# FFN inner units in three parts, and one pool of 4 KB buffers for weights and activations

## The chip, the cores and the metric

The kernel runs on one core of a Trainium2 chip. The metric is the device time of one execution in microseconds (us); of the kernel before there are three timed runs and one profiled execution. The engines are PE (TensorE: matrix products), PEld (its weight loads, which overlap PE), DVE (VectorE), ACT (ScalarE), POOL (GpSimd) and SP (SyncE, which here issues the DMAs).

## What is computed

A trunk of two layers over 256 latent tokens (stream L) and 256 context tokens (stream C) of 1024 features. Each layer is a feed forward, a token mixer (retention in layer 0, 2-D neighbourhood attention in layer 1) and a second feed forward:

```python
def ada_in(h, g, m, j):
    xn = rms_norm(h, g)
    return xn * (1.0 + m[:, j, 1][:, None]) + m[:, j, 0][:, None]

def gated_residual(h, m, j, y, w):
    return h + w * m[:, j, 2][:, None] * y

def swiglu(x, w_in, w_out):                 # w_in 1024 x 5632, w_out 2816 x 1024
    a, b = jnp.split(x @ w_in, 2, axis=-1)
    return (jax.nn.silu(a) * b) @ w_out

for i in range(2):
    h = gated_residual(h, ml, 0, swiglu(ada_in(h, norm_g[i, 0], ml, 0), ffn_w_in[i, 0], ffn_w_out[i, 0]), 0.5)
    ...
    h = gated_residual(h, ml, 1, yl, 1.0)   # yl: the mixer
    ...
    h = gated_residual(h, ml, 2, swiglu(ada_in(h, norm_g[i, 2], ml, 2), ffn_w_in[i, 1], ffn_w_out[i, 1]), 0.5)
return rms_norm(h, final_norm_g)
```

The context stream hc goes through the same steps with its own modulation (`mc`) and the same weights, up to the keys and values of layer 1's mixer. The output is the latent stream.

## The kernel before

**Stages.** `trunk()` lays the work out in one order, by hand: start-up (0 to 57 us of the profiled execution), FFN0 (57 to 412), retention (412 to 800), FFN1 (800 to 1192), FFN2 (1192 to 1555), neighbourhood mixer (1555 to 1750), FFN3 on the latent stream alone (1750 to 1945), final norm. All activations are kept transposed, features on the partitions, so that a product has 512 columns for both streams or 256 for one.

**Products.** Each matrix product is made as three: a weight and an activation are each split into a high part (a cast to fp32r, on ACT) and a low part (the rest, a subtraction on DVE), and PE adds up high·high, high·low and low·high (`acc3`, `acc3_part`, `mm`, which is the line L259 of the profile). L151 is the helper through which every instruction of DVE, ACT and POOL goes.

**Weights.** `plan` lists the weight tiles in the order of their use. `load()` issues a tile's DMA into a `raw` buffer, `prep()` queues the split into `whi` (ACT) and `wlo` (DVE) in two halves, `weight()` takes a tile, `retire()` gives its buffers back, and `pump()` starts what the free buffers allow. `wpool` has 2 `raw`, 3 `whi` and 3 `wlo` buffers of 8 KB per partition; activations live in 24 `slots` of 4 KB (160 KB in all).

**A feed forward** (`ffn`) goes over the 2816 inner units as 22 chunks of 128 in two parts of `HALF` = 11. In a part, 11 `win` tiles are multiplied (48 products each: `a` and `b` halves of the chunk, 8 k-blocks, 3 terms), each followed by silu, product and split (`gated_part`), and then 8 `wout` tiles, one for each output block n of 128 features, with 11 x 3 products each. `finish` adds an output block to h (`residual`: a DVE operation `h<-one,gate,h` for each stream); in the last part it is followed by the square of the new h (ACT) for the next norm.

**The hand-over.** In the last part of FFN0, FFN1 and FFN2 the blocks n = 6 and 7 are multiplied for one stream at a time, with 256 columns: L6, L7, C6, C7. When L7 is done, `chain` brings the L stream to the next stage: h, its square, the sum of the squares over the features (a product with a matrix of ones, 128x2, "rows product"), eight small DVE operations for the reciprocal root (`few`), two diagonal matrices (DVE), a product that spreads them over the partitions (128x128, "diagonal product"), and for each k-block of 128 features a scaled h on DVE (`t<-h,scl,one`), its high part on ACT and its low part on DVE (`slot<-t,modT,slot`). Meanwhile PE multiplies C6 and C7. Then the same follows for C, while PE multiplies the next stage's first products with L.

**Order.** Steps off the path are put in queues (`later`, `soon`, `due`), from which `advance()`, called after each product, takes what is due by a planner's clock `now`. The modulation of all layers (`bg`: `acc<-mraw,sT,acc` on DVE) runs in the background, one step for each `BG_EVERY` = 2.2 us.

Of the kernel before, what the change touches and what calls it, by code (L numbers as in the profile page):

```python
# [9 lines left out]
F32 = mybir.dt.float32  # L10
F32R = mybir.dt.float32r
# [13 lines left out]
HALF = NHC // 2  # L25
# [4 lines left out]
H_RET = 4  # L30
BIG = 1e30

# [39 lines left out]
def trunk(ctx, tc, a):  # L72
# [4 lines left out]
    slots = ctx.enter_context(tc.tile_pool(name="slots", bufs=24))  # L77
# [111 lines left out]

    plan = []  # L190

    def plan_all():
        for f in range(2):
            for hf in range(2):
                plan.extend(a["win"][f, hf * HALF + t] for t in range(HALF))
                plan.extend(a["wout"][f, hf, n] for n in range(KC))
            if f == 0:
                for hd in range(H_RET):
                    plan.extend([a["rq"][hd], a["rk"][hd], a["rv"][hd, 0], a["rv"][hd, 1]])
                    if hd:  # L200
                        plan.extend([a["ro"][hd - 1, 0], a["ro"][hd - 1, 1]])
                    plan.extend([a["rg"][hd, 0], a["rg"][hd, 1]])
                plan.extend([a["ro"][H_RET - 1, 0], a["ro"][H_RET - 1, 1]])
        for f in range(2, 4):
            for hf in range(2):
                plan.extend(a["win"][f, hf * HALF + t] for t in range(HALF))
                plan.extend(a["wout"][f, hf, n] for n in range(KC))
            if f == 2:
                for g in range(4):
                    plan.extend([a["nq"][g], a["nk"][g], a["nv"][g]])  # L210
                plan.extend(a["no"][n] for n in range(4))

    plan_all()
    RAWS, SPLITS = 2, 3
    raws, split_tiles = [], []
    state = {"loaded": 0, "freed": 0, "split": 0, "retired": 0, "bg_at": 0.0, "hold": True, "sums": True, "inside": True, "lag": (0.0, 0.0), "tight": False}
# [11 lines left out]
    def advance():  # L228
# [4 lines left out]
        while soon and not state["tight"] and soon[0][0] <= now["pe"] and ready_at(soon[0][5]) <= now["pe"] + 0.3 and free("dve", 0.5):  # L233
            soon.pop(0)[2]()
# [34 lines left out]
    def load():  # L269
        src = plan[state["loaded"]]  # L270
# [1301 lines left out]
```

## Time and profile before

| | us |
|---|---|
| timed runs, median of 3 (lowest to highest) | 1951.85 (1951.35 to 1952.06) |
| profiled execution, its own time | 1952.25 |
| its span | 1950.2 |
| PE busy | 1924.2 |
| DVE busy | 1352.0 |
| ACT busy | 687.9 |

The profiled execution is 0.40 us above the median, and 2.05 us of its time lie around the span. PE's busy time counts matmuls whose ends overlap the next one's start; starts of successive products tell the cadence better than the lengths.

### The profile page before, as it was taken

What the parts mean: (1) busy time and instruction counts of PE and PEld (TensorE: products, weight loads), DVE (VectorE), ACT (ScalarE), POOL (GpSimd) and SP (SyncE); (2) the same over time, 40 slices, a digit from 0 to 9 for tenths busy, and PEclk for the clock granted to TensorE, in tenths of its full rate; (3) what the DMA queues carried; (4) which work ended last, traced back from release to release, by engine and by line L of the source; (5) the groups of instructions that cost most, each with busy time, mean ns of one, the idle gap of its engine ahead of it and who ended that gap; (6) DMA issues with size and microseconds to landing.
All of it is one profiled execution on the core that took longest, in us unless ns stands there. A gap on an engine that the chain in (4) does not pass through costs nothing.

```text
span 1950.2 us, 26148 instructions
## 1 busy us (share of the span) xinstructions
PE 1924.2 (99%) x10458; PEld 1661.8 (85%) x10458; DVE 1352.0 (69%) x2402; ACT 687.9 (35%) x1035; POOL 73.0 (4%) x108
## 2 busy tenths in 40 slices
PE   7999999999999999999999999999999999999998
PEld 4888888898888888888888889888888899989998
DVE  5576666678788888876666676767632588887665
ACT  5422232333323232342222223322222366665443
POOL 1000000010000000100000000000000101100000
PEclk8999999999999999999999999999999999999999
DMA  7334534434434434234353343555433345544553
GB/s 287 141 137 129 187 130 136 156 119 151 142 133 141 147 130 142 86 130 149 125 179 132 140 139 98 194 189 200 162 101 82 110 119 113 98 115 167 194 176 114
DMA packets 70090, 278.85 MB, mean 143 GB/s; under 512 B 23632, under 2 KB 23888, under 8 KB 52304
## 3 DMA queue, kind: packets, MB, share of 16 engines
q1 hardware_dynamic: 69968, 277.18, 43.5%
q8 instruction: 82, 1.34, 0.3%
q14 instruction: 40, 0.33, 0.0%
HBM read 276.11 MB, written 1.05 MB: 142 GB/s over the span
## 4 chain that ended last, share of the span: by engine, by line
PE 94%; DVE 3%; ACT 2%; DMA 1%; issue 0%; SPq 0%; DVEq 0%; ACTq 0%
PE pair L259 61%; PE one L259 32%; DVE slot L151 1%; PE one L265 1%; DMA slot<-in_wmod 1%; DVE t L151 1%; ACT slot L151 1%; DVE wlo L151 1%; ACT whi L151 1%; DVE few L151 0%; DMA raw<-in_nv 0%; ACT t L151 0%; DVE h L151 0%; PE pair L265 0%; SPq L166 0%
## 5 line engine op out<-in xcount | busy, mean ns | idle before, releaser
L259 PE MATMUL pair<-slot,whi 128*128 128x512 f32 (+2 forms) x4000 | 1039.1, 351 | 6.8 <-ACT slot L151 4.7
L259 PEld LDWEIGHTS pair<-slot,whi 128*128 128x128 f32 x4000 | 696.4, 190 | 104.3 <-ACT slot L151 5.4
L259 PE MATMUL pair<-slot,wlo 128*128 128x512 f32 (+2 forms) x2000 | 682.5, 350 | 0.1
L259 PE MATMUL one<-slot,whi 128*128 128x512 f32 (+1 forms) x1860 | 481.4, 347 | 0.0
L151 DVE TENSOR_TENSOR wlo<-raw,whi 128x1024 fp32r<-128x1024 f32 (+1 forms) x400 | 436.4, 1122 | 38.5 <-ACT whi L151 37.7
L151 ACT CAST whi<-raw 128x1024 fp32r<-128x1024 f32 (+1 forms) x400 | 365.0, 959 | 225.3 <-PE one L259 138.6
L259 PEld LDWEIGHTS pair<-slot,wlo 128*128 128x128 f32 x2000 | 372.9, 190 | 48.8 <-DVE wlo L151 0.4
L259 PEld LDWEIGHTS one<-slot,whi 128*128 128x128 f32 x1860 | 325.9, 189 | 43.4
L259 PE MATMUL one<-slot,wlo 128*128 128x512 f32 (+1 forms) x930 | 323.1, 347 | 0.0
L151 DVE SCALAR_TENSOR_TENSOR acc<-mraw,sT,acc 128x512 f32<-128x512 f32 x392 | 279.2, 750 | 17.1 <-DMA mraw<-in_wmod 15.9
L151 ACT ACTIVATE t<-pair 128x512 f32<-128x512 f32 x66 | 39.4, 597 | 442.9 <-PE pair L259 442.9
L259 PEld LDWEIGHTS one<-slot,wlo 128*128 128x128 f32 x930 | 176.1, 189 | 21.8
L151 DVE TENSOR_TENSOR t<-pair,t 128x512 f32<-128x512 f32 x66 | 45.6, 692 | 204.2 <-ACT t L151 204.2
L151 DVE TENSOR_TENSOR slot<-t,slot 128x512 fp32r<-128x512 f32 (+2 forms) x144 | 88.1, 612 | 64.8 <-ACT slot L151 63.4
L151 ACT CAST slot<-t 128x512 fp32r<-128x512 f32 (+2 forms) x144 | 79.4, 552 | 122.1 <-DVE t L151 121.7
L151 DVE SCALAR_TENSOR_TENSOR h<-one,gate,h 128x256 f32<-128x256 f32 x112 | 49.6, 479 | 103.6 <-PE one L259 103.4
L151 POOL TENSOR_TENSOR t<-t,t 128x256 f32<-128x256 f32 x47 | 39.4, 850 | 1708.4 <-ACT t L151 1286.9
L259 PE MATMUL pair<-whi,slot 128*128 128x512 f32 (+1 forms) x384 | 98.5, 339 | 0.0
L259 PE MATMUL one<-slot,slot 128*128 128x512 f32 (+1 forms) x432 | 89.8, 348 | 1.3 <-DVE slot L151 1.0
L151 ACT ACTIVATE t<-h 128x256 f32<-128x256 f32 (+1 forms) x88 | 36.9, 434 | 142.8 <-DVE h L151 129.3
L259 PEld LDWEIGHTS one<-slot,slot 128*128 128x128 f32 x432 | 69.9, 189 | 10.8 <-DVE slot L151 1.4
L259 PEld LDWEIGHTS pair<-whi,slot 128*128 128x128 f32 x384 | 67.2, 189 | 7.5
(100 smaller groups left out, 1077.8 us busy)
## 6 DMA issues: line engine op xcount, KB each, us to landing
raw<-in_win SPq DMA_DIRECT2D x88, 1024.0 KB, 4.9
mraw<-in_wmod SPq DMA_DIRECT2D x128, 512.0 KB, 4.7
raw<-in_wout SPq DMA_DIRECT2D x64, 704.0 KB, 4.2
slot<-in_wmod SPq DMA_DIRECT2D x16, 512.0 KB, 10.3
raw<-in_rv SPq DMA_DIRECT2D x8, 1024.0 KB, 4.8
raw<-in_rg SPq DMA_DIRECT2D x8, 1024.0 KB, 4.9
raw<-in_ro SPq DMA_DIRECT2D x8, 1024.0 KB, 4.9
slot<-in_ex SPq DMA_DIRECT2D x8, 512.0 KB, 6.0
```

Source lines behind the costliest of these rows:

```text
L151: getattr(self.real, op)(*args, **kw)
L259: nc.tensor.matmul(out, lhsT=lhsT, rhs=rhs, start=start, stop=stop)
L265: nc.tensor.transpose(out=out, in_=in_, identity=ident)
```

## The change

The inner units of each feed forward go in three parts of 8, 7 and 7 chunks (`PARTS`) in place of two of 11. A part has again 8 output blocks, so each FFN adds to h three times, and the blocks of the last part have 7 x 3 products in place of 11 x 3. `wpool`'s weight buffers are gone: `slots` has 40 buffers of 4 KB (again 160 KB), shared by raw tiles (`RAWS` = 4 units at a time), split weights (`SPLITS` = 12) and activations. A `win` tile is loaded as two DMAs of 512 KB, a `wout` tile as one of 512 or 448 KB (the host lays `wout` out by chunk); SP issues 599 DMAs in place of 431.

The change brings a second way to multiply a tile (`Seven`, `product`, `seven`, `low_by_dma`), taken where `in_seven` is true. With `STANDARD` = (22, 22, 22) it is true for no tile. `operands(xt)`, which prepares the sums of activations that `seven` would read, is called in the last part of FFN0, FFN1 and FFN2 (`t1 == standard`), and nothing reads what it makes: in each FFN 8 additions of 512 columns, 3 combinations and 4 low parts of 1024 columns on DVE, and 4 casts of 1024 columns on ACT.

Two smaller edits: the background modulation takes one step for each 1.2 us until the block (0, C, 5) is made, and 2.2 us after that; `mcol` makes a missing modulation block on demand.

```diff
-HALF = NHC // 2
+PARTS = ((0, 8), (8, 15), (15, 22))
...
+SLOTS, RAWS, SPLITS = 40, 4, 12
...
+STANDARD, AMONG = (22, 22, 22), (2, 3, 3)
...
-    slots = ctx.enter_context(tc.tile_pool(name="slots", bufs=24))
+    slots = ctx.enter_context(tc.tile_pool(name="slots", bufs=SLOTS))
...
+    def in_seven(f, t):
+        return f < 3 and t >= STANDARD[f] and (t - STANDARD[f]) % AMONG[f] < AMONG[f] - 1
...
+    def plan_ffn(f):
+        for p, (t0, t1) in enumerate(PARTS):
+            for t in range(t0, t1):
+                if in_seven(f, t):
+                    plan.append(("seven", [a["wrow"][f, t, r] for r in range(2)]))
+                else:
+                    plan.append(("plain", halves(a["win"][f, t])))
+            plan.extend(("plain", [a["wout"][f, n][:, t0:t1, :]]) for n in range(KC))
...
         if not state["hold"] and now["pe"] >= state["bg_at"] and free("dve", 0.2):
-            state["bg_at"] = max(state["bg_at"], now["pe"] - 4 * BG_EVERY) + BG_EVERY
+
+            every = BG_EVERY if (0, C, 5) in made else 1.2
+            state["bg_at"] = max(state["bg_at"], now["pe"] - 4 * every) + every
             next(bg, None)
...
+        units = []
+        for src in srcs:
+            n = src.shape[1] * src.shape[2]
+            t = slots.tile([P, 1024], F32, tag="slot", name=nm("raw"))
+            dma(out=t[:, :n].rearrange("p (k c) -> p k c", k=src.shape[1]), in_=src)
+            units.append(t)
...
+    def part_tile():
+        return slots.tile([P, 1024], F32R, tag="slot", name=nm("wp"))
...
+    def operands(xt):
...
+        whole(0, L)
+        whole(0, C)
+        whole(1, C)
+        combine(1, (0, L), "minus", (0, L), (0, C))
+        two(1)
+        combine(3, (0, C), "minus", (1, C), (0, C))
+        combine(2, (1, C), "opposite", 1, (1, C))
+        two(2)
+        whole(1, L)
+        two(3)
+        combine(4, (1, L), "opposite", 2, (1, L))
+        two(4)
...
-        for hf in range(2):
+        for hf, (t0, t1) in enumerate(PARTS):
             gts = []
+            size, final = t1 - t0, hf == len(PARTS) - 1
...
+            if not raw and t1 == standard:
+                made_operands = operands(xt)
...
-            last = KC - 2 if hf == 1 and len(streams) == 2 else KC
+            last = KC - 2 if final and len(streams) == 2 else KC
...
                     for n, w in zip((KC - 2, KC - 1), ws):
                         ps = one()
-                        acc3(ps[:, xc], terms(w, xc, range(HALF)))
+                        acc3(ps[:, xc], terms(w, xc, range(size)))
```

By the instruction order, PE has 10278 matmuls in place of 10350: in each of FFN0, FFN1 and FFN2 48 products of 256 columns have become 24 of 512, since fewer of them are made for one stream alone. The columns multiplied are the same in all.

PE, where FFN0 hands over to retention. Before, `one_3095` is C7 (block 7 of stream C), and the diagonal product `one_3108` is put behind the first 4 of its 33 products:

```order
L259 MATMUL one_3095<-slot_1838,whi_2893 128x256 x2
L259 MATMUL one_3095<-slot_1838,wlo_2894 128x256
L259 MATMUL one_3095<-slot_1910,whi_2893 128x256
L259 MATMUL one_3108<-t_428_3071,con 128x128 x2
L259 MATMUL one_3095<-slot_1910,whi_2893 128x256
L259 MATMUL one_3095<-slot_1910,wlo_2894 128x256
L259 MATMUL one_3095<-slot_1991,whi_2893 128x256 x2
L259 MATMUL one_3095<-slot_1991,wlo_2894 128x256
```

After, `one_3243` is C7; its last products, the diagonal product `one_3303`, and then retention's first product `pair_3293`:

```order
L283 MATMUL one_3243<-slot_2812,wp_2970 128x256 x2
L283 MATMUL one_3243<-slot_2812,wp_2971 128x256
L283 MATMUL one_3243<-slot_2890,wp_2970 128x256 x2
L283 MATMUL one_3243<-slot_2890,wp_2971 128x256
L283 MATMUL one_3303<-t_551_3262,con 128x128 x2
L283 MATMUL pair_3293<-slot_3295,wp_3052 128x256
L283 MATMUL pair_3293<-slot_3296,wp_3052 128x256
L283 MATMUL pair_3293<-slot_3295,wp_3053 128x256
```

Before, 29 products of C7 stood behind the diagonal product; now none does, and 16 stand between the rows product and the diagonal product.

DVE, the same place. Before: from block 5 (`one_2901`) over L6 (`one_2956`) and L7 (`one_2998`) to the reciprocal root (`few`):

```order
L151 SCALAR_TENSOR_TENSOR h_84<-one_2901,gate_1441,h_84 128x256
L151 SCALAR_TENSOR_TENSOR h_85<-one_2901,gate_1443,h_85 128x256
L151 TENSOR_TENSOR wlo_2949<-raw_2878,whi_2948 128x1024
L151 SCALAR_TENSOR_TENSOR h_84<-one_2956,gate_1441,h_84 128x256
L151 TENSOR_TENSOR wlo_2949<-raw_2878,whi_2948 128x1024
L151 SCALAR_TENSOR_TENSOR h_84<-one_2998,gate_1441,h_84 128x256
L151 TENSOR_TENSOR t_372_2682<-t_423_3037,t_372_2682 128x256
L151 TENSOR_SCALAR few_3061<-one_3058 128x2
```

After: the same stretch, from block 5 (`one_3098`) over L6 (`one_3151`), L7 (`one_3181`) and C6 (`one_3212`); `slot_3118` and `slot_3130` belong to `operands`, `wp_3142` and `wp_3144` are low parts of weights:

```order
L161 SCALAR_TENSOR_TENSOR h_84<-one_3098,gate_1256,h_84 128x256
L161 SCALAR_TENSOR_TENSOR h_85<-one_3098,gate_1268,h_85 128x256
L161 TENSOR_TENSOR slot_3130<-slot_2937,slot_3129 128x1024
L161 SCALAR_TENSOR_TENSOR h_84<-one_3151,gate_1256,h_84 128x256
L161 SCALAR_TENSOR_TENSOR slot_3118<-slot_2946,slot_3118 128x1024
L161 TENSOR_TENSOR wp_3142<-raw_3107,wp_3141 128x1024
L161 SCALAR_TENSOR_TENSOR h_84<-one_3181,gate_1256,h_84 128x256
L161 TENSOR_TENSOR t_495_2962<-t_542_3210,t_495_2962 128x256
L161 TENSOR_TENSOR wp_3144<-raw_3109,wp_3143 128x1024
L161 SCALAR_TENSOR_TENSOR h_85<-one_3212,gate_1268,h_85 128x256
L161 TENSOR_SCALAR few_3252<-one_3249 128x2
```

An operation of `operands` and the low part of a weight now stand ahead of L7's `h_84`, and a weight's low part and C6's `h_85` ahead of `few`.

PE, where FFN1 hands over to FFN2. Before, `one_9315` is C7 and `one_9328` the diagonal product:

```order
L259 MATMUL one_9315<-slot_8069,whi_9113 128x256 x2
L259 MATMUL one_9315<-slot_8069,wlo_9114 128x256
L259 MATMUL one_9315<-slot_8147,whi_9113 128x256
L259 MATMUL one_9328<-t_1291_9291,con 128x128 x2
L259 MATMUL one_9315<-slot_8147,whi_9113 128x256
L259 MATMUL one_9315<-slot_8147,wlo_9114 128x256
L259 MATMUL one_9315<-slot_8227,whi_9113 128x256 x2
```

After, `one_9716` is C7, `one_9745` the diagonal product and `pair_9766` FFN2's first product:

```order
L283 MATMUL one_9716<-slot_9282,wp_9442 128x256 x2
L283 MATMUL one_9716<-slot_9282,wp_9443 128x256
L283 MATMUL one_9716<-slot_9362,wp_9442 128x256
L283 MATMUL one_9745<-t_1612_9709,con 128x128 x2
L283 MATMUL one_9716<-slot_9362,wp_9442 128x256
L283 MATMUL one_9716<-slot_9362,wp_9443 128x256
L283 MATMUL pair_9766<-slot_9737,wp_9518 128x256
L283 MATMUL pair_9766<-slot_9738,wp_9518 128x256
```

Before, 29 products of C7 stood behind the diagonal product; now 2 do. FFN2 into the neighbourhood mixer has the same form.

## Rows read from the trace of the kernel before

**Rows 1.** The page: span, engines and the granted clock in 40 slices.

```profile
span 1950.2 us, 26148 instructions
...
PE 1924.2 (99%) x10458; PEld 1661.8 (85%) x10458; DVE 1352.0 (69%) x2402; ACT 687.9 (35%) x1035; POOL 73.0 (4%) x108
...
PEclk8999999999999999999999999999999999999999
```

**Rows 2.** Windows: from:to, length, busy time (instructions) by engine, granted clock, DMA share, GB/s.

```profile
0.00:57.00 57.00, 45.82 (x197) 25.72 (x198) 31.50 (x66) 28.32 (x41) 8.61 (x29) 0.88 0.68 259
...
243.00:352.00 109.00, 109.00 (x485) 90.27 (x484) 70.68 (x116) 29.67 (x40) 0.00 (x0) 1.00 0.39 134
1555.00:1755.00 200.00, 194.93 (x1425) 182.45 (x1424) 167.90 (x342) 127.07 (x236) 26.70 (x35) 1.00 0.49 109
...
1847.00:1907.00 60.00, 60.00 (x499) 60.00 (x498) 40.10 (x62) 28.01 (x42) 0.00 (x0) 1.00 0.54 178
```

**Rows 3.** Timeline of PE, FFN0 into retention: start, length, instruction and count.

```profile
404.70 0.40 PE L259 MATMUL one<-slot,whi 128*128 128x256 f32 x2
...
406.74 0.51 PE L259 MATMUL one<-con,t 128*128 128x2 f32 x4
...
409.58 0.60 PE L259 MATMUL one<-t,con 128*128 128x128 f32 x4
...
413.49 0.40 PE L259 MATMUL pair<-slot,whi 128*128 128x256 f32 x2
```

**Rows 4.** Timeline of DVE, the same stretch, with idle time before and releaser.

```profile
404.90 0.48 DVE L151 SCALAR_TENSOR_TENSOR h<-one,gate,h 128x256 f32<-128x256 f32 x1 [2.34 <-PE one L259]
406.00 0.43 DVE L151 TENSOR_TENSOR t<-t,t 128x256 f32<-128x256 f32 x1 [0.61 <-ACT t L151]
407.28 0.16 DVE L151 TENSOR_SCALAR few<-one 128x2 int32<-128x2 int32 x1 [0.86 <-PE one L259]
...
410.22 0.87 DVE L151 SCALAR_TENSOR_TENSOR t<-h,scl,one 128x256 f32<-128x256 f32 x2 [0.36 <-PE one L259]
...
413.70 0.49 DVE L151 SCALAR_TENSOR_TENSOR h<-one,gate,h 128x256 f32<-128x256 f32 x1 [0.35 <-PE one L259]
...
417.85 0.48 DVE L151 SCALAR_TENSOR_TENSOR slot<-t,modT,slot 128x256 fp32r<-128x256 f32 x1 [0.18 <-ACT slot L151]
```

**Rows 5.** Timeline of ACT, the same stretch: the square of h.

```profile
405.48 0.42 ACT L151 ACTIVATE t<-h 128x256 f32<-128x256 f32 x1 [3.54 <-DVE h L151]
```

**Rows 6.** Timeline of DVE, FFN1 into FFN2.

```profile
1183.30 0.49 DVE L151 SCALAR_TENSOR_TENSOR h<-one,gate,h 128x256 f32<-128x256 f32 x1 [2.34 <-PE one L259]
...
1196.23 0.48 DVE L151 SCALAR_TENSOR_TENSOR slot<-t,modT,slot 128x256 fp32r<-128x256 f32 x1 [0.18 <-ACT slot L151]
```

**Rows 7.** Groups by line and shape: count, busy us, mean ns, idle before, releasers.

```profile
L151 DVE TENSOR_TENSOR wlo<-raw,whi 128x1024 fp32r<-128x1024 f32 x272 | 324.3, 1222 | 21.5 <-ACT whi L151 21.0
L151 DVE SCALAR_TENSOR_TENSOR acc<-mraw,sT,acc 128x512 f32<-128x512 f32 x392 | 279.2, 750 | 17.1 <-DMA mraw<-in_wmod 15.9
...
L151 DVE TENSOR_TENSOR slot<-t,slot 128x512 fp32r<-128x512 f32 x98 | 67.8, 692 | 56.8 <-ACT slot L151 56.3
...
L151 DVE SCALAR_TENSOR_TENSOR h<-one,gate,h 128x256 f32<-128x256 f32 x112 | 49.6, 479 | 103.6 <-PE one L259 103.4
...
L151 DVE TENSOR_TENSOR slot<-slot,slot 128x1024 fp32r<-128x1024 f32 x10 | 11.8, 1219 | 1.5 <-ACT slot L151 1.4
```

**Rows 8.** The page: the DMA issue of win, and weight loads of PE on low parts.

```profile
L259 PEld LDWEIGHTS pair<-slot,wlo 128*128 128x128 f32 x2000 | 372.9, 190 | 48.8 <-DVE wlo L151 0.4
...
raw<-in_win SPq DMA_DIRECT2D x88, 1024.0 KB, 4.9
```

**Rows 9.** Windows, columns as in rows 2: start of the kernel, neighbourhood into FFN3.

```profile
40.00:50.00 10.00, 9.06 (x36) 5.76 (x35) 10.00 (x11) 6.28 (x8) 0.00 (x0) 0.61 0.00 0
...
1733.00:1755.00 22.00, 18.02 (x136) 16.44 (x135) 19.66 (x52) 12.88 (x32) 1.62 (x2) 1.00 0.28 96
```

**Rows 10.** Timeline of DVE near the end of the neighbourhood mixer.

```profile
1738.52 2.34 DVE L151 TENSOR_TENSOR wlo<-raw,whi 128x1024 fp32r<-128x1024 f32 x2
```

More of the change, by code (lines that the diff above doesn't have):

```diff
@@ new lines, in plan_all @@
+    def plan_all():
+        two = lambda *srcs: plan.extend((MIXED and "mixed" or "plain", halves(x)) for x in srcs)
+        plan_ffn(0)
+        for hd in range(H_RET):
+            two(a["rq"][hd], a["rk"][hd], a["rv"][hd, 0], a["rv"][hd, 1])
+            if hd:
+                two(a["ro"][hd - 1, 0], a["ro"][hd - 1, 1])
+            two(a["rg"][hd, 0], a["rg"][hd, 1])
+        two(a["ro"][H_RET - 1, 0], a["ro"][H_RET - 1, 1])
+        plan_ffn(1)
+        plan_ffn(2)
+        for g in range(4):
+            two(a["nq"][g], a["nk"][g], a["nv"][g])
+        two(*(a["no"][n] for n in range(4)))
+        plan_ffn(3)
@@ L232, in advance @@
         go(later[L])
-        while soon and not state["tight"] and soon[0][0] <= now["pe"] and ready_at(soon[0][5]) <= now["pe"] + 0.3 and free("dve", 0.5):
+        while soon and not state["tight"] and soon[0][0] <= now["pe"] and ready_at(soon[0][5]) <= now["pe"] + 0.3 and free("dve", 0.5) and state["parts"] + soon[0][6] <= SPLITS:
             soon.pop(0)[2]()
@@ L277, in prep, with landed @@
+    def landed(n):
+        state["raw"] -= n
+        pump()
     def prep():
[L278 removed]
+        kind, units, srcs = raws.pop(0)
         tile_no = state["split"]
         state["split"] += 1
[L281 to L296 removed]
@@ L300, in pump, with released @@
+    def released(n):
+        state["parts"] -= n
+        pump()
     def pump():
         while True:
-            if raws and state["split"] - state["retired"] < SPLITS:
+            if raws and (not split_tiles if raws[0][0] == "seven" else
+                         state["parts"] + 2 * len(raws[0][1]) <= state["limit"] and not any(x[6] for x in soon)):
                 prep()
-            elif state["loaded"] < len(plan) and state["loaded"] - state["freed"] < RAWS:
+            elif state["loaded"] < len(plan) and state["raw"] + len(plan[state["loaded"]][1]) <= RAWS:
@@ L446, in mcol @@
         c0 = (j * 3 + w) * KC
-        assert all((l, v, (c0 + k) // 4) in made for k in range(kk.start, kk.stop))
+        while not all((l, v, (c0 + k) // 4) in made for k in range(kk.start, kk.stop)):
+            if due:
+                mod_sum(*due.pop(0)[1])
+            else:
+                next(bg, None)
         return modT[:, l, v, c0 + kk.start:c0 + kk.stop]
@@ L782, in ffn @@
                 state["hold"] = False
-            for t in range(len(gts), HALF):
+            for t in range(len(gts), size):
+                if t0 + t == standard:
+                    x7 = made_operands()
+                    state["limit"] = SPLITS
+                if in_seven(2 * l + which, t0 + t):
+                    gts.append(slot([P, 2, 512], F32R))
+                    seven(t, gts[t], x7)
+                    continue
+                if not raw and t0 + t == standard - 3 and standard < PARTS[0][1]:
+                    made_operands = operands(xt)
+                if t0 + t == standard - 3 and standard == PARTS[0][1]:
+                    state["limit"] = SPLITS - 4
                 wh, wl = weight()
```

254 lines of the change are left out of this document (193 added, 61 removed).

## Prediction

> **What bounds the kernel now.** The page's table of engines comes first: PE is busy for 1924.2 of 1950.2 us, DVE for 1352.0 [rows 1]. Busy time does not say whether PE could go faster, so the cadence is read next from windows in which nothing else can matter. In 243:352, all products with 512 columns, 484 weight loads lie in 109.00 us, 225.2 ns for each; in 1847:1907, all with 256 columns, 499 matmuls lie in 60.00 us, 120.2 ns [rows 2]. So two products of 256 columns cost 240.4 ns and one of 512 costs 225.2 ns: the columns are PE's price, and splitting them adds 15.2 ns.
>
> Counted by this cadence, PE loses little anywhere. Start-up (0:57) has 45.82 us of PE work in it, the neighbourhood mixer (1555:1755) 194.93 of 200.00 [rows 2], and of the latter 4.0 us lie in 1733:1755 [rows 9]. The change leaves PE's columns alone. So the questions are: where does the change take cover away from a chain that PE waits for, and is there a gap that it closes?
>
> The chain to look at is the hand-over between stages. At FFN0 into retention, call T the moment when L7 ends, 404.70, where C6's products begin [rows 3]. Then h of block 7 (404.90), its square on ACT (405.48), the addition (406.00), the rows product (406.74), the eight small operations (from 407.28), the diagonal product (409.58), the scaled h (410.22), and so on until the last low part of L begins at 417.85 and ends at 418.33, T + 13.63 [rows 3 to 5]. PE meanwhile does C6 and C7, 66 products, and reaches retention's first product at 413.49, T + 8.79 [rows 3]: 66 x 0.1202 = 7.93, and 0.86 for the two small products. The next stage begins with 48 products on L alone, k-block by k-block, six for each, 5.77 us, so without a stall PE is through them at T + 14.56. It can't be before the last low part's end and five more products, T + 13.63 + 0.60 = T + 14.23. So the chain is hidden, by 0.3 us. FFN1 into FFN2 reads the same: h at 1183.30 (so T = 1183.10), last low part 1196.23 to 1196.71, T + 13.61 [rows 6].
>
> **The change part by part.**
>
> Cover at the three hand-overs. C6 and C7 have 2 x 7 x 3 = 42 products in place of 66. PE is at the next stage's first product 24 x 0.1202 = 2.88 us earlier, at T + 5.91, and would be through its 48 at T + 11.68. The chain behind T is a chain of DVE, ACT and two small PE products, and no link of it gets shorter but one: the wait of 0.35 us for C7's h at 413.70 [rows 4], since C7 is done earlier. At FFN1 into FFN2 and FFN2 into the neighbourhood mixer I get T + 13.63 - 0.35 + 0.60 = T + 13.88, a stall of 2.2 us. DVE's new order puts one more low part of a weight (1.222 us [rows 7]) between h of L7 and the addition, in a gap of 0.61 us [rows 4], so 0.4 more is likely: 2.6 us each.
>
> FFN0 into retention gets more. The order puts a low part of a weight and C6's h ahead of the small operations. C6's h can't run before C6 ends at T + 21 x 0.12 = T + 2.5; behind the low part it is done by about T + 3.9, where the small operations began at T + 2.58 before (407.28 [rows 4]). That is 1.3 us later, 0.9 more than in the other two: 3.5 us.
>
> Bounds for one hand-over: 1.0 us if the operations of C in L's chain (two h, one addition, about 1.1 us by their starts) move out of it; 4.5 us if an operation of `operands` (1.219 us [rows 7]) lies in it besides. Three of them: 3.0 to 13.5, and I take 2.6 + 2.6 + 3.5 = 8.7.
>
> Fewer, longer products. 144 products of 256 columns become 72 of 512: 72 x 15.2 ns = 1.1 us gained [rows 2]. The skill has another price: the Trainium skill, "TensorE: Matmul & The Clock Gate", section "Back-to-back issue gap", gives N / 2.4 + 2.5 ns for an isolated matmul, by which the 72 would give back 0.18 us, and the sum be 0.9 us longer. It puts a product of 512 columns at 216 ns; the trace has 225.2 in a row of 484, so the measurement decides.
>
> A third part. Each of the four FFNs adds its output to h once more: DVE's h operations grow from 112 to 168, 56 x 0.479 = 26.8 us [rows 7], beside PE. In a two-stream part, an output block lasts 21 x 0.2252 = 4.7 us on PE (24 in the first part: 5.4), and DVE has two h (0.96) and the low part of 896 or 1024 columns (at most 1.222) to do in it, and at times a few modulation steps of 0.750 [rows 7]: hidden. In FFN3 a block lasts 2.5 us and needs 1.7. From `win` to `wout`, PE has the six other chunks of the first two blocks, 2 x 6 x 3 x 0.2252 = 8.1 us in place of 13.5, while the last chunk's gate needs about 3: hidden. In FFN3 it is 4.3 us in place of 7.2, against some 3.6: just hidden, 0 to 1 us. Nothing is taken.
>
> Dead work. `operands` adds 8 operations of 512 columns (0.692 us) and 7 of 1024 (1.219) to DVE in each of three FFNs [rows 7]: 3 x 14.1 = 42 us. They run in the last part beside `wout`: DVE has 8 blocks of 4.7 us there, 38 us, with 8 x (0.96 + 1.1) = 16 us of its own. 14 fit, but they are queued behind one another, and what isn't done by L7 lands in the chain, which is the upper bound above. With the h operations DVE goes from 1352 to about 1420 us, far below PE.
>
> Loads. SP issues more DMAs, of half the size; 1024 KB landed in 4.9 us in the median, and PE's loads of low parts waited 0.4 us in all for DVE [rows 8], so weights are early. 40 buffers of 4 KB hold what 24 and 8 of 8 KB held. Nothing taken, -1 to +1 us.
>
> Faster background. In FFN0's first part a step each 1.2 us means 9 steps in a `win` tile of 48 x 0.2252 = 10.8 us: 9 x 0.750 = 6.8 on DVE, with 2.4 for the low parts and 1.4 for the gate 10.6 us. That is all but full; 0 to 2 us, I take 0.3.
>
> Sum: 8.7 - 1.1 + 0.3 = +7.9 us. The profiled execution would go from 1952.25 to 1960.15; it is 0.40 above the median, so the forecast for the median is **1959.8 us**. With all bounds on one side: 3.0 - 1.1 - 1.0 = +0.9, and 13.5 - 1.1 + 1 (FFN3) + 1 (loads) + 2 (background) = +16.4, so 1952.8 to 1968.3; all of them together are unlikely.
>
> **Rivals.**
>
> (a) The hand-overs stay nearly hidden: DVE takes C's operations behind L's, and stalls are 0.6 us each. 1.8 - 1.1 + 0.3 = +1.0, 1952.9. For it: DVE idles for 2.34 us before L7's h and 0.86 before the small operations [rows 4], so there is room. Against: the cover falls by 2.88 us and the slack was 0.3; the chain itself is of fixed length.
>
> (b) Faster, by one mechanism: the pool. At the neighbourhood's end DVE does two low parts of weights in a row, 2.34 us at 1738.52 [rows 10], just ahead of L's last blocks, and PE is busy for 18.02 of 22.00 us [rows 9]. Deeper splits could take these ahead of time. If all 4.0 us went and the hand-overs cost nothing: -1.1 + 0.3 - 4.0 = -4.8, 1947.1. It decides only where the hand-overs are hidden wholly. Against: the order of DVE there is almost what it was.
>
> (c) Worse: the dead work and the faster background push DVE behind by several operations. Two dead operations more in each chain, 3 x 2 x 1.2 = +7.3 on the forecast: about 1967.
>
> (d) The clock. PE was granted 0.61 of its full speed in 40:50, a mean of its two levels, 1.2 and 2.4 GHz [rows 9], in a start-up with 45.82 us of work in 57 [rows 2], and 1.00 in 1733:1755 in spite of 4.0 idle us. If each stall brought ten such microseconds, 3 x 10 x 0.39 = 11.7 us came on top: 1971.5. The Trainium skill, "TensorE: Matmul & The Clock Gate", section "HAM oscillation — how this bites in real kernels", tells of kernels whose PE falls to the lower clock at each wait for data; the row of 1733:1755 speaks against it here.
>
> (e) The change does something else than it says. By the order `seven` is never used and all products are plain, as said; only `operands` runs for nothing, and is in the sum.
>
> **How the numbers follow.** A measurement can tell about 0.2%, 3.9 us, from no change: 1947.95 to 1955.75. The forecast's mechanism has 0.62, nearly all of it slower than that bound; (a) 0.19, (b) 0.06, (c) 0.10, (d) 0.03. Slower: 0.62 + 0.10 + 0.03 = 0.75; same 0.19; faster 0.06. The range goes from (a)'s lower side, 1951.5, to half of the way between the forecast and the upper bounds, 1964.5; (b), (c) and (d) stay out.
>
> **What would show it.** In the profile after, windows around the three hand-overs should have PE idle for 2 to 4 us each, with PE's first products released by DVE's and ACT's slots of L (pair<-slot, whi), and the row of 1024-column slot operations on DVE some 24 longer; the clock at 1.00 there. Stretches inside a part should keep 225 ns. It would be wrong if the hand-overs show no idle time, if a new wait for DMA stands in the middle of an FFN, or if the idle time in 1733:1755 is gone.

## The result, and the profile after

The changed kernel takes 1970.58 us in the median of four runs (1967.79 to 1974.28), the kernel before 1951.60 in the same series. The ratio is 1.0098, with a 95% interval of 1.0078 to 1.0118: slower by 19 us, where 8 were forecast (1959.8, in a range of 1951.5 to 1964.5). The profiled execution took 1968.56 us, with a span of 1966.5, 16.3 us longer than before [rows 1]. The four runs lie in two pairs, 1967.8 and 1968.6 at a mean granted clock of 0.991, 1972.6 and 1974.3 at 0.988, and the median lies between them, so a difference to it is uncertain by up to the 4 us of that interval.

The page of the kernel after, its engines:

```profile
PE 1929.7 (98%) x10386; PEld 1663.2 (85%) x10386; DVE 1414.9 (72%) x2474; ACT 695.3 (35%) x1015; POOL 88.0 (4%) x108
```

DVE's busy time is what the sum of its new operations gave (1414.9, about 1420 forecast). One group of the trace of after, by line and shape (count, busy us, mean ns, idle before, releasers), is needed below: POOL's additions of squares, which took 850 ns each before.

```profile
L161 POOL TENSOR_TENSOR t<-t,t 128x256 f32<-128x256 f32 x47 | 53.7, 1155 | 1713.7 <-ACT t L161 1692.9 <-DVE t L161 20.2
```

The loss lies at the three hand-overs. PE's timeline at FFN0 into retention (start, length, instruction, count, and in brackets the idle time before it with its releaser):

```profile
404.72 6.40 PE L283 MATMUL one<-slot,wp 128*128 128x256 f32 x52
413.23 0.61 PE L283 MATMUL one<-con,t 128*128 128x2 f32 x4 [2.11 <-DVE t L161]
413.69 2.16 PE L283 MATMUL one<-slot,wp 128*128 128x256 f32 x16
416.99 0.71 PE L283 MATMUL one<-t,con 128*128 128x128 f32 x4 [1.14 <-DVE t L161]
419.83 7.78 PE L283 MATMUL pair<-slot,wp 128*128 128x256 f32 x38 [2.13 <-ACT slot L161]
427.45 0.51 PE L283 MATMUL one<-con,t 128*128 128x2 f32 x4
```

The 52 products of 256 columns from 404.72 on are the last 5 of L6, L7, C6 and 5 of C7. At 0.1202 us each [rows 2] they are issued by 410.97, so L7 ends 26 products earlier, at T = 407.85. The rows product comes at T + 5.38 (T + 2.04 before [rows 3]), retention's first product at 419.83, T + 11.98, where the forecast had T + 5.91 if nothing waited. And the next 38 products take 7.62 us to the rows product of C at 427.45, where 38 x 0.1202 = 4.57: 3.05 more without any wait in between, at a lower clock (below). So 6.07 + 3.05 = 9.1 us are lost here, where 3.5 were forecast.

DVE at the same place, from L6's h to L7's, and then the last low part of L:

```profile
408.29 0.47 DVE L161 SCALAR_TENSOR_TENSOR h<-one,gate,h 128x256 f32<-128x256 f32 x1
408.69 1.37 DVE L161 SCALAR_TENSOR_TENSOR slot<-slot,slot 128x1024 f32<-128x1024 f32 x1
409.98 1.76 DVE L161 TENSOR_TENSOR wp<-raw,wp 128x1024 fp32r<-128x1024 f32 x1
411.66 0.47 DVE L161 SCALAR_TENSOR_TENSOR h<-one,gate,h 128x256 f32<-128x256 f32 x1
...
425.21 0.48 DVE L161 SCALAR_TENSOR_TENSOR slot<-t,modT,slot 128x256 fp32r<-128x256 f32 x1 [0.18 <-ACT slot L161]
```

L7 ends at 407.85, and its h starts at 411.66, after an operation of `operands` (408.69, 1.37 us) and the low part of a weight (409.98, 1.76 us, while POOL was adding squares beside it). DVE's queue was late before that: L6 ends 21 products earlier, at 405.33, and its h starts 2.96 us later, at 408.29. Before, h followed 0.20 us after the end of L7 [rows 3, 4]. The last low part ends at 425.69, T + 17.84, where it was T + 13.63 before.

FFN1 into FFN2, PE:

```profile
1185.70 12.35 PE L283 MATMUL one<-slot,wp 128*128 128x512 f32 x83
1199.38 0.58 PE L283 MATMUL one<-con,t 128*128 128x2 f32 x4 [1.32 <-DVE t L161]
...
1203.26 1.05 PE L283 MATMUL one<-t,con 128*128 128x128 f32 x4
...
1205.43 1.49 PE L283 MATMUL pair<-slot,wp 128*128 128x256 f32 x7 [0.76 <-ACT slot L161]
1207.13 4.66 PE L283 MATMUL pair<-slot,wp 128*128 128x256 f32 x31 [0.21 <-DVE slot L161]
1211.63 0.50 PE L283 MATMUL one<-con,t 128*128 128x2 f32 x4
```

The 20 products ahead of the rows product's wait put T at 1195.51. FFN2's first product comes at 1205.43, T + 9.92, 4.0 late, and from there to 1211.63 38 products take 6.20 us, 1.6 more than 4.57: 5.6 us. Of the 4.0, some 1.4 are slow work of PE itself: from 1199.81 to the diagonal product 20 products take 3.45 us in place of 2.40, and the diagonal product takes 0.71 in place of the 0.36 that it takes at the third hand-over (1573.53 to 1573.89). FFN2 into the neighbourhood mixer, PE:

```profile
1557.62 11.67 PE L283 MATMUL one<-slot,wp 128*128 128x512 f32 x80
1570.62 0.58 PE L283 MATMUL one<-con,t 128*128 128x2 f32 x4 [1.33 <-DVE t L161]
...
1575.25 0.38 PE L283 MATMUL pair<-slot,wp 128*128 128x256 f32 x1 [0.88 <-ACT slot L161]
1576.00 0.98 PE L283 MATMUL pair<-slot,wp 128*128 128x256 f32 x6 [0.37 <-DVE slot L161]
1578.16 6.84 PE L283 MATMUL pair<-slot,wp 128*128 128x256 f32 x52 [1.19 <-DVE slot L161]
1584.84 0.51 PE L283 MATMUL one<-con,t 128*128 128x2 f32 x4
```

T = 1566.74, first product at T + 8.51, 2.6 late; 59 products take 9.59 us in place of 7.09, here with two waits for L's low parts between them: 5.1 us. The three together are 9.1 + 5.6 + 5.1 = 19.8, where the forecast had 8.7.

At the second and third, the last addition of squares is released by POOL. DVE and POOL at the second, and the last low parts of L at the second and third:

```profile
1196.43 0.47 DVE L161 SCALAR_TENSOR_TENSOR h<-one,gate,h 128x256 f32<-128x256 f32 x1
1196.83 1.36 DVE L161 TENSOR_TENSOR wp<-raw,wp 128x1024 fp32r<-128x1024 f32 x1
1198.81 0.42 DVE L161 TENSOR_TENSOR t<-t,t 128x256 f32<-128x256 f32 x1 [0.62 <-POOL t L161]
...
1211.53 0.48 DVE L161 SCALAR_TENSOR_TENSOR slot<-t,modT,slot 128x256 fp32r<-128x256 f32 x1 [0.18 <-ACT slot L161]
...
1582.23 0.48 DVE L161 SCALAR_TENSOR_TENSOR slot<-t,modT,slot 128x256 fp32r<-128x256 f32 x1 [0.18 <-ACT slot L161]
```

```profile
1194.02 4.75 POOL L161 TENSOR_TENSOR t<-t,t 128x256 f32<-128x256 f32 x3 [3.76 <-ACT t L161]
```

POOL's three additions of squares end at 1198.77, and DVE, done with L7's h and a low part by 1198.19, waits for them. The last low parts end at T + 16.50 and T + 15.97.

Windows of after (from:to, length, busy time by engine, granted clock, DMA share, GB/s):

```profile
415.00:420.00 5.00, 1.73 (x13) 1.34 (x11) 3.88 (x14) 1.36 (x4) 0.73 (x1) 0.94 0.34 105
420.00:425.00 5.00, 5.00 (x22) 4.76 (x23) 5.00 (x13) 3.06 (x7) 0.00 (x0) 0.50 0.01 3
1200.00:1205.00 5.00, 4.67 (x26) 4.45 (x25) 2.86 (x14) 0.54 (x2) 0.73 (x1) 0.66 0.58 171
1205.00:1210.00 5.00, 4.08 (x26) 3.44 (x27) 4.82 (x13) 3.21 (x7) 0.00 (x0) 1.00 0.71 252
```

In 415:420 PE is busy for 1.73 of 5 us; in 420:425 it is busy throughout, at a granted clock of 0.50, the lower of its two levels. At 1200:1205 it is 0.66, in the products ahead of the diagonal product; in 1205:1210, behind FFN2's first product, it is 1.00, so the 1.6 us there are not the clock's but waits for L's slots.

From the neighbourhood mixer on both kernels have the same products in nearly the same order, so they can be matched by their count, taken from the last. One product early in the mixer and one at its end, first before, then after (a row's start is that of its first product):

```profile
1576.18 0.40 PE L259 MATMUL one<-slot,whi 128*128 128x256 f32 x2
...
1741.81 0.84 PE L259 MATMUL pair<-slot,whi 128*128 128x256 f32 x2 [1.33 <-ACT slot L151]
```

```profile
1595.91 5.92 PE L283 MATMUL one<-slot,wp 128*128 128x256 f32 x48
...
1758.13 2.04 PE L283 MATMUL pair<-slot,wp 128*128 128x256 f32 x12 [0.27 <-ACT slot L161]
```

The first comes 19.7 us later than before, the second 16.3: 3.4 us are gained in the mixer, 2.0 of them at its hand-over into FFN3.

Sum: +19.8 at the hand-overs, -1.1 for fewer products (as forecast, not measured apart), some 1.0 more in FFN0 and retention, -3.4 in the neighbourhood mixer: 16.3, as the spans differ.

### The profile page after: what moved, and what is told of

Read it like the earlier page. It is cut to its first block, busy times and chain, and to the rows that moved or that the text cites. A ratio compares the mean times of both kernels' runs of the same rounds, so it can differ in the third digit from the quotient of the medians.

```text
span 1966.5 us, 26526 instructions
## 1 busy us (share of the span) xinstructions
PE 1929.7 (98%) x10386; PEld 1663.2 (85%) x10386; DVE 1414.9 (72%) x2474; ACT 695.3 (35%) x1015; POOL 88.0 (4%) x108
## 4 chain that ended last, share of the span: by engine, by line
PE 88%; DVE 7%; ACT 2%; issue 1%; DMA 1%; POOL 0%; SPq 0%; DVEq 0%; ACTq 0%; POOLq 0%
PE pair L283 60%; PE one L283 27%; DVE slot L161 2%; DVE wp L161 1%; DVE t L161 1%; PE one L289 1%; ACT slot L161 1%; DVE h L161 1%; DMA slot<-in_wmod 1%; ACT t L161 1%; DVE few L161 0%; DVE acc L161 0%; DMA mraw<-in_wmod 0%; DMA slot<-in_ex 0%; POOL t L161 0%
## 5 line engine op out<-in xcount | busy, mean ns | idle before, releaser
L283 PE MATMUL pair<-slot,wp 128*128 128x512 f32 (+2 forms) x6000 | 1150.2, 352 | 11.5 <-ACT slot L161 7.4
L283 PEld LDWEIGHTS pair<-slot,wp 128*128 128x128 f32 x6000 | 980.0, 191 | 159.2 <-ACT slot L161 8.8
L283 PE MATMUL one<-slot,wp 128*128 128x512 f32 (+1 forms) x2718 | 522.3, 353 | 0.0
L283 PEld LDWEIGHTS one<-slot,wp 128*128 128x128 f32 x2718 | 446.4, 190 | 67.7
L161 DVE TENSOR_TENSOR wp<-raw,wp 128x1024 fp32r<-128x1024 f32 (+1 forms) x368 | 433.1, 1206 | 24.8 <-ACT wp L161 22.6
L161 ACT CAST wp<-raw 128x1024 fp32r<-128x1024 f32 (+1 forms) x368 | 362.0, 1026 | 135.6 <-DMA raw<-in_win 64.3
L161 POOL TENSOR_TENSOR t<-t,t 128x256 f32<-128x256 f32 x47 | 53.7, 1155 | 1713.7 <-ACT t L161 1692.9
L283 PE MATMUL pair<-wp,slot 128*128 128x512 f32 (+1 forms) x576 | 104.6, 338 | 0.0
L283 PEld LDWEIGHTS pair<-wp,slot 128*128 128x128 f32 x576 | 89.8, 189 | 11.3
L161 ACT ACTIVATE slot<-t,modT 128x256 fp32r<-128x256 f32 x80 | 39.4, 507 | 58.0 <-DVE t L161 58.0
L161 DVE TENSOR_TENSOR slot<-slot,slot 128x512 f32<-128x512 f32 (+2 forms) x52 | 51.3, 1024 | 5.2 <-ACT slot L161 5.1
```

The lines of the kernel that those rows point to most:

```text
L161: getattr(self.real, op)(*args, **kw)
L283: nc.tensor.matmul(out, lhsT=lhsT, rhs=rhs, start=start, stop=stop)
```

## The experiments

All times are medians, beside runs of the kernel before on the same chip (1951.4 to 1951.6 in each series). e1 to e8, f1 to f4 and g1 start from the changed kernel, g2 and g3 from the kernel before. In the diffs "..." marks lines that are left out.

**e1: no dead work.**

```diff
-            if not raw and t1 == standard:
-                made_operands = operands(xt)
```

> The changed kernel without the calls of operands (its result is read by nothing; the output stays the reference's). Three parts and the pool stay. Theory A (the dead work makes DVE and POOL late at the last blocks, and that lies on top of the lost cover): the first hand-over falls from 10 us of idle or slow PE to about 3.5, the other two from 6 to about 2.6, the final addition no longer waits for POOL, and the time is 1957 to 1961. Theory B (the lost cover of 24 products bares a chain that is that long anyway): 1966 or more.

Measured: 1965.29 us (1963.69 to 1966.62), ratio 1.0070 (1.0055 to 1.0085). The dead work is 5.3 of the 19 us by the medians, 3.0 by the spans of the two profiled executions (1963.5 beside 1966.5), and the two intervals overlap a little; the time lies between the figures of the two theories, and both were missed. At FFN0 into retention DVE is late again, with other work in its place, and PE waits too:

```profile
410.34 0.48 DVE L161 SCALAR_TENSOR_TENSOR h<-one,gate,h 128x256 f32<-128x256 f32 x1
410.92 2.43 DVE L161 TENSOR_TENSOR wp<-raw,wp 128x1024 fp32r<-128x1024 f32 x2
413.27 0.47 DVE L161 SCALAR_TENSOR_TENSOR h<-one,gate,h 128x256 f32<-128x256 f32 x1
```

```profile
409.58 2.98 PE L283 MATMUL one<-slot,wp 128*128 128x256 f32 x23 [1.01 <-DVE h L161]
```

L7's products end at about 408.3 here, so its h is 4.9 us late. Between h of L6 and h of L7 stand both low parts of the next tile, 2.43 us, and the blocks of 7 chunks leave 21 x 0.12 = 2.5 us between the two; L6's h was 4.5 us late already, behind background steps of 0.75 us, which filled DVE. The row of PE is C6's first product: it waits 1.01 us until DVE has taken a late block out of its PSUM tile (by the releaser; not tried by itself).

**e2: two parts again, with the dead work.** `wout` tiles of 11 chunks come as two units.

```diff
-PARTS = ((0, 8), (8, 15), (15, 22))
+PARTS = ((0, 11), (11, 22))
...
+            mid = t0 + min(8, (t1 - t0 + 1) // 2) if t1 - t0 > 8 else t1
...
```

> The changed kernel with two parts of 11 chunks again, operands still called; a wout tile of 11 chunks is loaded as units of 6 and 5. Theory A: the cover of 66 products hides a part of the lateness, 1953 to 1957. Theory B: all is hidden as before, 1950 to 1953.

Measured: 1952.99 us (1950.35 to 1956.19), ratio 1.0009 (1.0000 to 1.0018). With everything else of the change in place, two parts take 17.6 us of the 19 away. Theories A and B touch at 1953, so it does not tell them apart.

**e3: two parts, no dead work.** The edits of e1 and e2.

> Two parts of 11 and no operands: what is left of the change is the pool of 4 KB buffers, the smaller loads and the faster background. Both theories expect 1949 to 1953; if the pool or the loads cost anything by themselves, it is above 1954.

Measured: 1957.23 us (1955.18 to 1958.55), ratio 1.0031. This missed, and is 4 us slower than with the dead work: in the retention mixer PE waits 4.2 us ahead of a modulation sum (at 623.4), and the granted clock is 0.72 in the 5 us behind it. The same kind of wait is shown for f1 below.

**e4: filler products.** 24 products of C behind C7, into a PSUM tile that nothing reads.

```diff
                     done(s)
+                idle = one()
+                for _ in range(24):
+                    mm(idle[:, xc], lhsT=ws[-1][0][:, 0, :], rhs=gts[0][:, 0, xc], start=True, stop=True)
```

> The changed kernel with 24 more products of 256 columns behind C7 in each of the three hand-overs; their sums go to a PSUM tile that nothing reads. They stand where PE is idle. Theory C (after a stall PE's granted clock is at its lower level for some microseconds, 4.8 us in the profiled run and twice that in others): the clock stays higher behind the hand-overs and the time is 1963 to 1967, with less scatter. If the clock costs nothing: 1968 to 1972.

Measured: 1967.59 us (1965.32 to 1969.28), ratio 1.0082; 72 products more and 3.0 us less, just above the range for theory C and below that for a clock that costs nothing. Two windows at the first hand-over:

```profile
410.00:415.00 5.00, 4.67 (x27) 4.68 (x27) 4.44 (x14) 0.49 (x2) 0.73 (x1) 0.66 0.37 126
...
420.00:425.00 5.00, 5.00 (x42) 4.92 (x41) 4.42 (x16) 2.04 (x4) 0.00 (x0) 1.00 0.13 48
```

The clock is 1.00 in 420:425 where it was 0.50. The waits ahead of the rows product, where no filler stands, stay, and behind the first of them the clock falls now: 0.66 in 410:415. So the filler gives back 3.0 us by the medians, but the intervals of the two kernels overlap, and what all of the lower clock costs it does not show. (By the windows of after the lower level lasted some 10 us at the first two hand-overs together, not 4.8; of the other runs no trace exists.)

**e5: sums of squares on DVE.**

```diff
-            step = lambda: (G_ if n < (4 if brisk else KC - 1) else V).tensor_tensor(out=acc, in0=sq, in1=acc, op=ALU.add)
+            step = lambda: (G_ if n < 4 else V).tensor_tensor(out=acc, in0=sq, in1=acc, op=ALU.add)
```

> The changed kernel with one edit: of the sum of squares of the new h, blocks 4 to 6 are added on DVE too (as block 7 is), only blocks 2 and 3 on POOL. Theory D (at FFN1 into FFN2 and FFN2 into the neighbourhood mixer the last addition waits for POOL, whose three additions take 4.75 us there, and PE waits 1.3 us each for it): these two waits of PE for the rows product go, 2 to 4 us less than the changed kernel, 1966 to 1969. If POOL only came last by chance and DVE is as late by itself: 1969 to 1973.

Measured: 1971.11 us (1970.44 to 1971.15), ratio 1.0100. Theory D falls. The waits for POOL are gone at FFN1 into FFN2, and PE waits as long at the next links:

```profile
1199.16 0.61 PE L283 MATMUL one<-con,t 128*128 128x2 f32 x4
...
1203.42 1.05 PE L283 MATMUL one<-t,con 128*128 128x128 f32 x4 [1.87 <-DVE t L161]
1206.19 6.02 PE L283 MATMUL pair<-slot,wp 128*128 128x256 f32 x31 [1.72 <-ACT slot L161]
```

The rows product is not late any more, but a low part, C's h and C's sum now run on DVE ahead of the small operations; the diagonal product waits 1.87 us, the first product 1.72. POOL came last, but DVE's queue behind it was as late. Matched product by product with the changed kernel, the second and third hand-over are 1.1 and 1.8 us longer and the first 2.4 shorter; and at retention into FFN1, where the edit puts additions on DVE too, 3.3 us are lost.

**e6: more cover, three parts and dead work as they are.** Blocks 5, 6 and 7 for one stream at a time.

```diff
-            last = KC - 2 if final and len(streams) == 2 else KC
+            last = KC - 3 if final and len(streams) == 2 else KC
...
-                ws = [weight(), weight()]
+                ws = [weight() for _ in range(3)]
...
-                    for n, w in zip((KC - 2, KC - 1), ws):
+                    for n, w in zip(range(KC - 3, KC), ws):
...
```

> The changed kernel, three parts and the dead work as they are, but blocks 5, 6 and 7 of the last part are multiplied for one stream at a time (L5, L6, L7, C5, C6, C7), so that 63 products cover L's chain in place of 42. If the cover is the cause: the hand-overs hide nearly all again and the time is 1953 to 1957, like two parts with the dead work. If it is the shorter blocks that make DVE late (7 chunks, 2.5 us for L6 and L7 each), the first hand-over keeps 3 to 6 us: 1958 to 1963.

Measured: 1960.62 us (1959.38 to 1961.18), ratio 1.0045. 63 products of cover in place of 42 give 10.0 us back, of the 19; the first hand-over keeps its lateness, and the time is the second case's: the cover is not all of it.

**e7: two parts, no dead work, slow background.** e3 with

```diff
-            every = BG_EVERY if (0, C, 5) in made else 1.2
+            every = BG_EVERY
```

> Two parts, no operands, and the background at one step per 2.2 us throughout: what is left is the pool and the smaller loads. In the run of two parts without operands one wait of 4.5 us stood in the retention mixer, where PE waits for a modulation sum. If the faster background put it there: 1950 to 1953. If it stays: 1955 to 1958.

Measured: 1949.47 us (1948.73 to 1950.82), ratio 0.9989 (0.9980 to 0.9999). What is left is the pool and the smaller loads, which were not tried apart, and it is faster than the kernel before by 2.2 us. The product at the mixer's end again:

```profile
1738.78 2.02 PE L284 MATMUL pair<-slot,wp 128*128 128x256 f32 x12 [0.27 <-ACT slot L161]
```

It comes 3.0 us earlier than before (1741.81), and early in the mixer e7 was level with the kernel before: this gain belongs to the pool with its loads, as in the kernel after.

**e8: three parts, no dead work, slow background.** e1 with the edit of e7.

> Three parts, no operands, background at 2.2 us throughout. In the run without operands background steps had taken the place of the dead work ahead of L7's h. If any work put there makes DVE late, taking both away gives 1958 to 1962; if the two low parts of weights and the lost cover do it alone: 1963 to 1966.

Measured: 1972.19 us (1971.84 to 1974.20), ratio 1.0108, a miss on the other side: slower than with the fast background. With FFN0's shorter blocks the slow background comes too late; PE waits 3.6 us ahead of a modulation sum at 149.8, and DVE does background steps at the first hand-over.

**f1: deeper splits.** e1 with

```diff
-SLOTS, RAWS, SPLITS = 40, 4, 12
+SLOTS, RAWS, SPLITS = 40, 4, 14
```

> Three parts, no operands, fast background, and 14 units of split weights at a time in place of 12, so that in the order both low parts of the next stage's second tile stand ahead of L6's block and no longer between h of L6 and h of L7. If they are what makes L7's h late at FFN0 into retention (3.5 us in the run with 12 units): 1960 to 1963. If anything else fills DVE there, or the lost cover alone decides: 1964 to 1967.

Measured: 1965.16 us (1964.01 to 1966.62), ratio 1.0071, no change in all, which is the second case's figure, but for another reason. Counted by PE's starts, as above, the three hand-overs fell by about 5 us together (retention's first product came at 416.89 in place of 421.10), and one wait in retention, with a granted clock of 0.63 in the 5 us behind it (630:635), took it back:

```profile
627.60 0.63 PE L283 MATMUL one<-small,con 128*128 128x32 f32 x2 [3.38 <-DVE t L161]
```

The releaser is a `t` of DVE, not the sum's own input: four PSUM tiles (`one`) serve these products, and the sum waits until DVE has read one of them. That it is the PSUM tile was not tried by itself.

**f2: more cover, no dead work.** The edits of e1 and e6.

> Three parts, no operands, blocks 5 to 7 for one stream at a time (63 products of cover). Theory of two causes that add (lost cover 10 us, dead work 5 us): 1953 to 1957. If background steps take the dead work's place ahead of L7 again: 1957 to 1961.

Measured: 1953.66 us (1951.60 to 1954.27), ratio 1.0011 (1.0002 to 1.0020). Both causes taken away leave 2.2 us of the 19. PE's waits at the first hand-over are down to 0.79 us ahead of one of L's products, and 1.13 for the rows product:

```profile
408.00 0.61 PE L283 MATMUL one<-con,t 128*128 128x2 f32 x4 [1.13 <-DVE t L161]
```

**f3: cover halved, nothing else.** e7, with block 7 alone for one stream at a time (`KC - 1`): 33 products of cover, blocks as long as before.

> Two parts of 11, no operands, slow background (1949.5 us as it was), but only block 7 is multiplied for one stream at a time: the blocks are as long as before and DVE has no more to do, only the cover falls, from 66 products to 33. By the prediction's arithmetic each hand-over then costs 33 x 0.12 = 4.0, less 0.3 of slack and 0.35 for C's h, 3.3 us, and 1 to 2 more where the clock falls; 1.5 us come back for 99 fewer products: 1957 to 1963. If the cover is not what costs, but DVE's lateness with short blocks: under 1954.

Measured: 1962.18 us (1961.80 to 1962.99), ratio 1.0055 (1.0038 to 1.0071): 12.7 us more than e7, as the arithmetic of the cover said. At FFN1 into FFN2, PE:

```profile
1196.81 0.68 PE L284 MATMUL one<-t,con 128*128 128x128 f32 x4 [0.98 <-DVE t L161]
1199.49 6.51 PE L284 MATMUL pair<-slot,wp 128*128 128x256 f32 x38 [2.00 <-ACT slot L161]
```

and at FFN0 into retention two windows:

```profile
410.00:415.00 5.00, 2.40 (x19) 2.03 (x17) 3.37 (x15) 0.61 (x2) 0.00 (x0) 0.95 0.97 316
415.00:420.00 5.00, 4.64 (x20) 4.41 (x21) 4.82 (x13) 3.25 (x7) 0.00 (x0) 0.50 0.21 80
```

The diagonal product waits 0.98 us and the first product 2.00, 3.0 in all beside 3.3 expected; then 38 products take 6.35 us. The clock is 0.50 in 415:420, and falls at the other two hand-overs too (0.70 in 1200:1205, 0.66 in 1570:1575). DVE is nearly in time: L7's h starts 0.97 us after its products, and the rows product does not wait. So cover alone costs in waits what the prediction's sum says, and the clock comes on top.

**f4: two parts, deeper splits.** e7 with 14 units.

> Two parts, no operands, slow background, 14 units of split weights: 1948 to 1950 if earlier splits shorten the neighbourhood's hand-over into FFN3 further, 1949 to 1951 if not.

Measured: 1949.65 us (1947.89 to 1950.27), ratio 0.9990 (0.9981 to 1.0000), the same as e7. e7 and f4 are the fastest kernels here.

**g1: the dead work alone.** e7, with `operands` called again.

> Two parts of 11, slow background (1949.5 us so far), and operands called again: the dead work alone, with the full cover of 66 products. If it costs only where the hand-over is bare: 1949 to 1951. If it costs by itself (DVE's time, POOL's slower additions): 1953 or more.

Measured: 1952.77 us (1951.39 to 1954.38), ratio 1.0008 (0.9998 to 1.0017). 3.3 us more than e7, between the two cases: PE waits 0.5 us for the rows product at the first hand-over, and 2.3 ahead of a modulation sum in retention, with the clock at 0.81 in the 5 us behind it (625:630). Matched product by product, 0.8 us of the difference arise at the first hand-over and 3.9 at that sum.

**g2 and g3: three parts alone, in the kernel before.** Its own buffers, `PARTS` as in the change, modulation blocks made on demand; g3 has the faster background too.

```diff
-HALF = NHC // 2
+PARTS = ((0, 8), (8, 15), (15, 22))
...
-        for hf in range(2):
+        for hf, (t0, t1) in enumerate(PARTS):
+            size, final = t1 - t0, hf == len(PARTS) - 1
...
```

> The kernel before with three parts alone: its own buffers of 8 KB, no operands, background at 2.2 us, a missing modulation block made on demand. If the parts are the cause and the pool, the dead work and the background are not: 1961 to 1967, with 4 to 8 us of PE's idle or slow time at each hand-over. If the pool has a share in it: 1955 to 1960.

> The same with the background at 1.2 us until the block (0, C, 5) is made. With FFN0's parts shorter the modulation has less room at 2.2 us; if its blocks made on demand cost PE waits in the run before, 2 to 5 us less than that; if not, the same within 2 us.

Measured: g2 1980.06 us (1976.50 to 1981.67), ratio 1.0145; g3 1979.07 (1977.38 to 1979.25), ratio 1.0142. Both cases put for g2 were missed: three parts alone are worse than the whole change, by 9.5 us, and worse by 14 than three parts with the pool and the same background (g3 beside e1). The pool has a share, with the sign opposite to the one that was put: it repays. DVE at FFN1 into FFN2 in g2:

```profile
1196.22 0.48 DVE L151 SCALAR_TENSOR_TENSOR h<-one,gate,h 128x256 f32<-128x256 f32 x1 [1.50 <-PE one L259]
1196.62 2.90 DVE L151 TENSOR_TENSOR wlo<-raw,whi 128x1024 fp32r<-128x1024 f32 x2
1199.44 0.47 DVE L151 SCALAR_TENSOR_TENSOR h<-one,gate,h 128x256 f32<-128x256 f32 x1
```

With three pairs of 8 KB, 2.90 us of low parts stand between h of L6 and h of L7. But the three hand-overs are not where the 14 us lie. Matched product by product, g3 loses against e1 4.1 us at a change of parts in FFN0 (384 to 400 us), 4.3 in the neighbourhood mixer and 5.8 in FFN3, and nothing at the three hand-overs together (-3.0, 0 and +2.0). In FFN0 and FFN3 PE waits for the splits of weights; in g2:

```profile
392.87 0.50 PE L259 MATMUL one<-slot,wlo 128*128 128x512 f32 x1 [2.49 <-DVE wlo L151]
...
1903.77 0.51 PE L259 MATMUL pair<-slot,whi 128*128 128x258 f32 x2 [1.00 <-ACT whi L151]
```

## Why the prediction was wrong

**Direction and place: right.** The lost cover of C6 and C7 bares a chain that PE waits for. Two parts instead of three took 17.6 of 19 us away (e2), 21 more products of cover took 10.0 away with three parts and the dead work kept (e6), and halving the cover of a kernel with two parts cost 12.7 (f3), within the range that the prediction's own arithmetic gave. The cover's own term, 2.2 us for each hand-over, is borne out by f3 (3.0 us of waits, 3.3 by the same sum).

**The size of that term: wrong, 8.7 forecast, 19.8 measured.** The step that failed is what stands on top of the cover in "2.6 us each" and "3.5 us": the lateness of L's chain, put at 0.4, 0.4 and 1.3 us, 2.1 in all. By the sum the last low part of L ends at T + 13.28 (13.63 less 0.35) and that much; it did at T + 17.84, T + 16.50 and T + 15.97, so the chain was late by 4.6, 3.2 and 2.7 us, 10.5 in all. With 3 x 2.2 for the cover that makes 17.1 of the 19.8; most of the rest lies at the first hand-over, where PE itself ran at the lower clock. It failed in three ways.

First, L7's h. The chain was timed from L7's end, and the lateness of its first link was taken from the gaps of the old trace: one low part in a gap of 0.61 us, 0.4 more. But the shorter blocks also shrink the time from L6's h to L7's, from 33 to 21 products, 1.4 us, while DVE's queue there grows: the order shown ahead of the prediction has an operation of `operands` and a low part ahead of L7's h, and the sum left that h where it was. In the trace h of L7 was 3.8 us late at the first hand-over, and h of L6 2.96 before it. With the dead work gone background steps and two low parts made L7's h 4.9 us late (e1). The prediction counted the dead work against a whole part of 38 us, and so did not see that a queue served in order is late wherever its last microseconds are full. The dead work cost 5.3 us with bare hand-overs (e1 beside after) and 7.0 with more cover (f2 beside e6); with full cover and slow background it cost 3.3, most of it at a modulation sum in retention (g1). Rival (c), DVE late by several operations, came nearest to this: +7.3 on the forecast, where the chain was 8.4 us later than put; it had a chance of 0.10 and stayed out of the range.

Second, POOL. That the squares of blocks 2 to 6 are added on POOL was nowhere in the sum, and at two hand-overs its last addition came after DVE's own work. e5 shows that this link was not what decided: without it, DVE's queue took as long at the next link.

Third, the clock, which had no term in the sum. Rival (d) had 0.03, on the row of 1733:1755, which keeps 1.00 with 4.0 idle us. There the idle time is spread over 22 us; at the first hand-over PE did 1.73 us of work in five, and the following five ran at 0.50. It came at two of three hand-overs: 3.05 us behind L's first product at the first, 1.4 ahead of the diagonal product at the second (which count in the 3.2 of its chain), at most 4.4 by the timelines; the filler (e4) gave back 3.0 by the medians, which is not clear of the scatter. So (d) was right in kind, at less than half of its price of 11.7. Behind that sentence: the Trainium skill, "TensorE: Matmul & The Clock Gate", section "What's actually happening", names two levels and says that the lower is the one of an engine that has been idle; the windows at 0.50 agree.

**The range.** The upper bounds added up to 1968.3 and were cut to 1964.5, "all of them together are unlikely". They are not independent: a late DVE lengthens the chain, and at two of the three bare hand-overs the clock fell. Half of the way to the upper bound is 1964.1, not 1964.5, which changes nothing. The profiled execution took 1968.56.

**What held.** The gain of rival (b) came, as a part of 4.0: 2.0 us into FFN3, 3.4 in the whole mixer, and 2.2 us in all for the pool (e7). Loads were not late; no stretch inside a part of the changed kernel waits for a DMA. That the pool and its loads would be neutral beside three parts was wrong in a way that the sum could not show: without them three parts cost 28.6 us (g2). The term for the faster background, 0.3, can't be told: with three parts slow was worse (e8), with two parts slow was better (e7 beside e3), in both cases mainly by a single wait ahead of a modulation sum and the lower clock behind it. Where such a wait falls was not settled.

## What to carry to other kernels

When a loop is cut finer, ask at each hand-over which products lie behind the last block, and add up the chain from that block's end: cover lost there is paid nearly in full, and filling engines that run in order up to that moment is paid again. Bounds that come from one cause, here a bare chain, a late queue and a lower clock, belong at the same end of the range together. Test a change's parts one by one, and in more than one company: here the pool with its loads gains 2 us, and the cut that came with it costs 17.6 beside the dead work (after and e2), 8.1 without it (e1 and e3) and 22.7 with the slow background (e8 and e7).

## What the runs showed of the hardware

POOL's additions of 256 columns took 850 ns in the mean before and 1155 after, and three in a row 4.75 us (1.6 each) while DVE ran operations with two inputs from SBUF; alone they took 0.73 us. DVE's low parts of 1024 columns took 1.35 and 1.76 us beside them in place of 1.22. The Trainium skill, "GPSIMD Engine Reference", section "1. Specifications", says that the two share their SBUF interfaces and contend when a DVE instruction has two inputs there; the trace agrees, and gives it a price.
